# Low parts of a seven-product unit's weight sums in one operation, and three more down units by seven products

## The chip, the cores and the metric

The kernel runs on one core of a Trainium2 chip. The metric is the device time of one execution in microseconds (us). The kernel before took 2016.33 us in the median of 3 runs (2015.55 to 2018.14).

## What is computed

A decoder trunk of two layers on 256 tokens with 2048 channels, in float32. Layer 0 mixes tokens by causal pooling, layer 1 by dilated attention with shared keys and values; each layer ends in a gated feed-forward block (FFN) and a layer norm. The change concerns the FFN, cut here to what matters:

```
def conv_ffn(h, w_up, conv_w, conv_b, w_down):
    S = h.shape[1]
    u = h @ w_up                                   # 2048 -> 2 x 5504
    ...
    gate, val = jnp.split(c, 2, axis=-1)           # c: u after a causal convolution of width 3
    return (jax.nn.silu(gate) * val) @ w_down      # 5504 -> 2048
```

## The kernel before

**Numbers in two parts.** The operands of the large products have the type float32r. Each is held as a high part (the number rounded to that type) and a low part (the rest), and a product of two operands is three matmuls: high by high, high by low, low by high. For a weight tile, ScalarE makes the high part `wh` by a copy and VectorE the low part `wl` by a subtraction. In `do_split` these are lines 99 and 100 of the kernel.

**Units.** All large products are cut into units, one unit for each weight tile of 512 rows by 512 columns (1 MB). A unit's life: SyncE's queue loads the tile into `raw` (3 buffers, line 89); the split makes `wh` and `wl` (4 buffers each); TensorE runs the unit's matmuls; post-processing follows where a sum is complete. `run_units` walks the list of units in order. Before the matmuls of unit i it issues loads up to unit i + 5 and the split of unit i + 3 (`ahead`), then the matmuls, then whatever was put off to this unit (`later`), then the post-processing. Each engine takes its own instructions in exactly this order, so the order of `ahead`, pending work and post-processing is the order of VectorE's and of ScalarE's queue.

**Plain units and seven-product units.** An up unit (lines 180 and 181) is 32 matmuls. A plain down unit (`go_t`, lines 255 to 257) is 24 matmuls of 512 columns: 4 blocks of 128 rows, 2 halves of the tokens, 3 matmuls each. A seven-product unit computes the same by a Strassen-like scheme with 7 block products in place of 8: 7 x 2 x 3 = 42 matmuls of 256 columns (lines 244 to 246). It needs sums of blocks of the weight tile and sums of blocks of the left operand, and it is two entries in the list of units:

- part "a" has the load. `split_sums(i, "a")` makes the high part of three blocks (ScalarE, line 119), the low part (VectorE, line 121), and turns the raw tile in place into the four sums of blocks (VectorE, lines 120, 122 and 124). Its matmuls are three of the seven products.
- part "b" has no load. `split_sums(i, "b")` splits these sums, in two halves of 256 columns, N2 and then N1: the high part by ScalarE (line 113), the low part by VectorE (line 114). N2 is complete after line 122, N1 after line 124. Its matmuls are the other four products, N2's first.

The sums of the left operand are made once for each quarter of the hidden units (512 of the 5504) by `left_sums`; the dictionary `sets` says which memory holds them. Products that leave the scheme go through `early_post` (lines 844 to 857), the rest through `tm_post` (lines 869 to 876), both adding to the tile `ht`.

**Which units use it.** In `ffn`, `sevens` says for each quarter q which of the four column groups of `w_down` go by seven products. Before, these are: in both layers quarters 0 to 6 at all columns and quarter 7 of layer 1 at all columns; quarter 7 of layer 0 at columns 0 and 1; quarter 9 of layer 1 at columns 0 and 2. Eight more units of the shared V projection use it too: 72 in all.

**Where they stand.** In each FFN, quarters 0 to 2 and 3 to 5 are woven into up units (`weave`): up, up, seven, up, seven, up, seven, and so on, so that one round is four plain units and three seven-product units (the woven stretches). Quarters 6 and 7 of each column stand together between groups of up units. Quarters 8 to 10 come last: in layer 0 as plain units in another order of operands, in layer 1 as down units that end the kernel, with the last layer norm behind them.

**Names on the other lines.** Line 607 and 608 collect the up products (`u`), lines 616 to 622 are the convolution, 844 to 876 the down products' additions, 901 to 951 the last norm.

Of the kernel before, what the change touches and what calls it, by code (L numbers as in the profile page):

```python
# [9 lines left out]
F32 = mybir.dt.float32  # L10
# [3 lines left out]
OP = mybir.AluOpType  # L14
# [18 lines left out]
def trunk(ctx: ExitStack, tc: tile.TileContext, x, pool_w_in, pool_w_grp, pool_scale, pool_w_out,  # L33
# [3 lines left out]
    V, A, PE = nc.vector, nc.scalar, nc.tensor  # L37
# [53 lines left out]
    def do_split(i):  # L91
        if len(units[i]) > 3:
            return split_sums(i, units[i][3])
        r = raw.pop(i)
        shape = [P, r.shape[1], r.shape[2]]
        wh[i] = wp.tile(shape, F32R, name=f"wh{i}", tag="wh")
        wl[i] = wp.tile(shape, F32R, name=f"wl{i}", tag="wl")
        for j, s in enumerate(pieces(i, r.shape[1])):
            A.copy(wh[i][:, s], r[:, s])  # L99
            V.tensor_tensor(wl[i][:, s], r[:, s], wh[i][:, s].bitcast(F32), OP.subtract)  # L100
            if i == 0 and j == 0:
                x_quad(0, (1,))


    B1, B2, N1, N2 = slice(0, 4, 2), slice(1, 4, 2), slice(256, 512), slice(0, 256)

    def split_sums(i, kind):
        h = wh[i] = wp.tile([P, 4, 512], F32R, name=f"wh{i}", tag="wh")
        l = wl[i] = wp.tile([P, 4, 512], F32R, name=f"wl{i}", tag="wl")
        if kind == "b":  # L110
            r = raw.pop(i - 1)
            for n in (N2, N1):
                A.copy(h[:, :, n], r[:, :, n])  # L113
                V.tensor_tensor(l[:, :, n], r[:, :, n], h[:, :, n].bitcast(F32), OP.subtract)  # L114
            return
        r = raw[i]
        r11, r12, r22 = r[:, B1, N1], r[:, B1, N2], r[:, B2, N2]
        hs, ls, rs = (t.rearrange("p (k b) n -> p k (b n)", b=2)[:, :, 256:] for t in (h, l, r))
        A.copy(hs, rs)  # L119
        V.tensor_tensor(r12, r12, r11, OP.subtract)  # L120
        V.tensor_tensor(ls, rs, hs.bitcast(F32), OP.subtract)  # L121
        V.tensor_tensor(r22, r22, r12, OP.subtract)  # L122
        both = r[:, :, N1].rearrange("p (k b) n -> p k b n", b=2)
        V.tensor_tensor(both, both, r22.unsqueeze(2).to_broadcast([P, 2, 2, 256]), OP.subtract)  # L124
# [455 lines left out]
    def ffn(lay):  # L580
# [5 lines left out]
        sevens = {q: every for q in range(8)}  # L586
        sets = {0: "C", 1: "A", 2: "B", 3: "C", 4: "A", 5: "B", 6: "A", 7: "CB"[lay], 9: "A"}
        if lay == 1:
            sevens[9] = (0, 2)
        else:  # L590
            sevens[7] = (0, 1)
        free, done = {}, {}

        def pads():
# [265 lines left out]
    def tm_post(lay, n, c):  # L860
# [92 lines left out]
        return post  # L953

    ffn(0)
    marks.append(len(units))

# [174 lines left out]
    add_last(attn_w_o[0], rows4, [lambda j=j: oq[j] for j in range(4)], True, 1, 0, after=to_tokens)  # L1132
    marks.append(len(units))
    ffn(1)
    marks.append(len(units))

# [34 lines left out]
    with tc.tile_pool(name="pool", bufs=1) as pp:  # L1171
# [5 lines left out]
        for l in range(2):  # L1177
            n = 80 if l == 0 else 64
            r = pp.tile([80, P], F32, name=f"vrow{l}")
# [94 lines left out]
```

## Time and profile before

| | |
|---|---|
| profiled execution, span | 2014.9 us |
| median of 3 runs | 2016.33 us |
| TensorE matmul busy | 2005.8 us, 12760 instructions |
| VectorE busy | 1734.9 us, 1831 instructions |
| ScalarE busy | 1269.7 us, 1551 instructions |
| DMA moved | 407.77 MB, mean 202 GB/s |

How to read it: the profile is one execution on the chip, and its span runs from the first to the last instruction. PE is TensorE's matmul, PEld its weight load, DVE VectorE, ACT ScalarE, POOL GpSimd, SP SyncE, which issues the loads. A matmul's row lasts longer than its share of the time, since matmuls overlap; what counts is the distance from one start to the next. "Idle before" is idle time of the engine ahead of an instruction, and the arrow names what ended it. A row of a timeline gives the start, the length, the engine, the line, the operation and the tiles (written from read).

### The profile page before, as it was taken

The numbers are of one execution on the slowest core, as the hardware profiler recorded it, in microseconds if no ns is written. First come the engines' busy times: TensorE is split into PE (matmuls) and PEld (weight loads), VectorE is DVE, ScalarE is ACT, GpSimd is POOL, SyncE is SP. The second block draws the span as 40 slices with busy tenths as digits, with TensorE's granted clock in tenths as the row PEclk, the third lists the DMA queues.
The fourth block names the chain that finished last, engine by engine and source line by source line (L and its number), as shares of the span: only waits on it lengthen the run. The fifth ranks groups of instructions, "written<-read, shape, count | busy, mean of one in ns | idle before, by whom it ended". The sixth has DMA issues, their size and how long they took to land.

```text
span 2014.9 us, 31474 instructions
## 1 busy us (share of the span) xinstructions
PE 2005.8 (100%) x12760; PEld 1810.2 (90%) x12760; DVE 1734.9 (86%) x1831; ACT 1269.7 (63%) x1551; POOL 93.0 (5%) x153
## 2 busy tenths in 40 slices
PE   9999999999999999999999999999999999999999
PEld 8898988999899988889888988998899989989987
DVE  6868887999899899879896878787899899989899
ACT  6454686767766676657554445487766677667673
POOL 2000000000000000000001021000000000000000
PEclk9999999999999999999999999999999999999999
DMA  8565466666666757885465656557666756666765
GB/s 260 204 208 186 163 212 192 181 221 223 198 198 200 239 179 229 232 230 186 155 220 172 210 172 202 187 188 211 166 224 200 224 186 222 209 211 186 213 208 185
DMA packets 271297, 407.77 MB, mean 202 GB/s; under 512 B 74430, under 2 KB 85588, under 8 KB 270896
## 3 DMA queue, kind: packets, MB, share of 16 engines
q1 hardware_dynamic: 259488, 388.93, 58.8%
q0 software_dynamic: 11232, 16.18, 5.4%
q8 instruction: 100, 1.64, 0.3%
q10 hardware_dynamic: 432, 0.66, 0.1%
q14 instruction: 45, 0.37, 0.1%
HBM read 380.01 MB, written 2.10 MB: 190 GB/s over the span
## 4 chain that ended last, share of the span: by engine, by line
PE 88%; DVE 7%; ACT 2%; DMA 2%; issue 1%; SPq 0%; DVEq 0%; ACTq 0%
PE acc L180 41%; PE acc L181 21%; PE s L244 3%; PE s L246 3%; PE s L245 3%; PE acc L184 2%; PE acc L185 2%; PE acc L183 2%; PE t L246 2%; PE t L244 2%; PE t L245 2%; DVE wl L100 2%; ACT wh L99 1%; DVE wl L114 1%; DVE wl L121 1%
## 5 line engine op out<-in xcount | busy, mean ns | idle before, releaser
L180 PE MATMUL acc<-xc,wh 128*128 128x512 f32 x3264 | 1151.6, 396 | 0.0
L181 PE MATMUL acc<-xc,wl 128*128 128x256 f32 x3264 | 916.2, 281 | 0.8 <-DVE wl L100 0.8
L100 DVE TENSOR_TENSOR wl<-raw,wh 128x2048 fp32r<-128x2048 f32 (+2 forms) x304 | 654.8, 2162 | 171.0 <-ACT wh L99 163.3
L180 PEld LDWEIGHTS acc<-xc,wh 128*128 128x128 f32 x3264 | 616.1, 189 | 142.8 <-issue 0.4
L99 ACT CAST wh<-raw 128x2048 fp32r<-128x2048 f32 (+2 forms) x304 | 546.6, 1805 | 170.8 <-PE acc L180 65.7
L181 PEld LDWEIGHTS acc<-xc,wl 128*128 128x128 f32 x3264 | 615.2, 188 | 1.3 <-DVE wl L100 1.2
L113 ACT CAST wh<-raw 128x1024 fp32r<-128x1024 f32 x144 | 150.7, 1052 | 202.8 <-DVE raw L122 175.5
L114 DVE TENSOR_TENSOR wl<-raw,wh 128x1024 fp32r<-128x1024 f32 x144 | 171.8, 1221 | 11.2 <-ACT wh L113 11.2
L121 DVE TENSOR_TENSOR wl<-raw,wh 128x1536 fp32r<-128x1536 f32 x72 | 126.2, 1753 | 6.3 <-ACT wh L119 5.3
L119 ACT CAST wh<-raw 128x1536 fp32r<-128x1536 f32 x72 | 106.4, 1477 | 36.6 <-PE acc L180 26.5
L287 POOL DMA_DIRECT2D ht<-w x48 | 41.3, 1015 | 1446.4 <-DVE ht L873 720.9
L244 PE MATMUL t<-wh,g 128*128 128x256 f32 x376 | 105.8, 281 | 0.0
L246 PE MATMUL t<-wh,g 128*128 128x256 f32 x376 | 105.7, 281 | 0.0
L245 PE MATMUL t<-wl,g 128*128 128x256 f32 x376 | 105.5, 281 | 0.0
L616 ACT ACTIVATE c<-u,cv 128x256 f32<-128x256 f32 x172 | 89.5, 593 | 23.2 <-DVE f L678 16.5
L246 PE MATMUL s<-wh,xs 128*128 128x256 f32 x344 | 96.1, 279 | 0.0
L244 PE MATMUL s<-wh,xs 128*128 128x256 f32 x344 | 95.9, 279 | 0.0
L245 PE MATMUL s<-wl,xs 128*128 128x256 f32 x344 | 95.9, 279 | 0.0
L124 DVE TENSOR_TENSOR raw<-raw 128x1024 f32<-128x1024 f32 x72 | 88.2, 1225 | 2.4
L621 ACT ACTIVATE a<-u,cv 128x256 f32<-128x256 f32 x172 | 73.5, 500 | 11.9 <-DVE g L688 11.9
L607 ACT COPY u<-acc 128x512 f32<-128x512 f32 x84 | 46.8, 572 | 46.1 <-PE acc L181 45.9
L621 ACT ACTIVATE u<-u,cv 128x256 f32<-128x256 f32 x172 | 73.4, 500 | 0.0
(338 smaller groups left out, 3443.1 us busy)
## 6 DMA issues: line engine op xcount, KB each, us to landing
raw<-in_ffn_w_up_dram SPq DMA_DIRECT2D x160, 1024.0 KB, 5.2
raw<-in_ffn_w_down_dram SPq DMA_DIRECT2D x80, 1024.0 KB, 5.1
raw<-in_pool_w_out_dram SPq DMA_DIRECT2D x16, 1024.0 KB, 5.0
raw<-in_shared_w_k_dram SPq DMA_DIRECT2D x16, 1024.0 KB, 5.2
raw<-in_attn_w_q_dram SPq DMA_DIRECT2D x16, 1024.0 KB, 5.3
raw<-in_shared_w_v_dram SPq DMA_DIRECT2D x16, 1024.0 KB, 5.4
raw<-in_attn_w_o_dram SPq DMA_DIRECT2D x16, 1024.0 KB, 5.2
ht<-w POOLq DMA_DIRECT2D x50, 256.0 KB, 4.8
```

The costliest lines, as they stand in the source:

```text
L99: A.copy(wh[i][:, s], r[:, s])
L100: V.tensor_tensor(wl[i][:, s], r[:, s], wh[i][:, s].bitcast(F32), OP.subtract)
L113: A.copy(h[:, :, n], r[:, :, n])
L114: V.tensor_tensor(l[:, :, n], r[:, :, n], h[:, :, n].bitcast(F32), OP.subtract)
L119: A.copy(hs, rs)
L121: V.tensor_tensor(ls, rs, hs.bitcast(F32), OP.subtract)
L180: PE.matmul(ps[m].ap, h[:, k, c], q[:, k, :, :T], start=st, stop=False)
L181: PE.matmul(ps[m][:, :T], l[:, k, c], q[:, k, 0, :T], start=False, stop=sp)
L244: PE.matmul(to, xh, h[:, k, n], start=opens and kk == 0, stop=False)
L245: PE.matmul(to, xh, l[:, k, n], start=False, stop=False)
L246: PE.matmul(to, xl, h[:, k, n], start=False, stop=ends and kk == 1)
L621: A.activation(to[:, m, :], u[:, m, i:i + T], AF.Copy, scale=cv[:, i, j:j + 1])
```

## The change

The split of part "b" is done in one operation on each engine instead of two halves, and three more down units go by seven products: quarter 7 of layer 0 at columns 2 and 3, quarter 9 of layer 1 at column 1. With all four columns of quarter 7 of layer 0 so computed, `left_sums` puts the fourth sum of that quarter into the part of the quarter's own tile that is not read any more, as for the other quarters.

```
         if kind == "b":
             r = raw.pop(i - 1)
-            for n in (N2, N1):
-                A.copy(h[:, :, n], r[:, :, n])
-                V.tensor_tensor(l[:, :, n], r[:, :, n], h[:, :, n].bitcast(F32), OP.subtract)
+            A.copy(h, r)
+            V.tensor_tensor(l, r, h.bitcast(F32), OP.subtract)
             return
...
         if lay == 1:
-            sevens[9] = (0, 2)
-        else:
-            sevens[7] = (0, 1)
+            sevens[9] = (0, 1, 2)
```

## The prediction

> **What bounds the kernel now.** I read the page first, then busy time by stretches, then groups of instructions by shape, then the timelines of VectorE, ScalarE and TensorE side by side.
>
> ```profile
> span 2014.9 us, 31474 instructions
> PE 2005.8 (100%) x12760; PEld 1810.2 (90%) x12760; DVE 1734.9 (86%) x1831; ACT 1269.7 (63%) x1551; POOL 93.0 (5%) x153
> ...
> PE 88%; DVE 7%; ACT 2%; DMA 2%; issue 1%; SPq 0%; DVEq 0%; ACTq 0%
> ...
> L181 PE MATMUL acc<-xc,wl 128*128 128x256 f32 x3264 | 916.2, 281 | 0.8 <-DVE wl L100 0.8
> ```
>
> TensorE has hardly a gap (the largest behind the start is the 0.8 us of the last row, where it waited for VectorE's L100), and the chain of waits runs through it for 88% of the span. So time is gained only by less TensorE work, and lost wherever another engine delivers late. VectorE's 86% hides how close it is; the stretches show that (columns: length, then busy time and count of PE, PEld, DVE, ACT, POOL, clock, DMA share, GB/s).
>
> ```profile
> 625.27:662.56 37.29, 37.29 (x256) 34.43 (x256) 35.67 (x33) 24.30 (x28) 1.72 (x2) 1.00 0.66 209
> 805.88:811.46 5.58, 5.58 (x27) 4.52 (x26) 3.32 (x5) 3.94 (x6) 0.00 (x0) 1.00 0.56 125
> 811.46:816.41 4.95, 4.95 (x44) 4.95 (x43) 3.11 (x3) 4.71 (x7) 0.00 (x0) 1.00 1.00 259
> ```
>
> The first row is one round of a woven stretch, three seven-product units and four plain ones: VectorE works 35.67 of 37.29 us. The other two are TensorE's time for one plain down unit (5.58) and one seven-product unit (4.95). The second engine has 1.6 us of slack a round.
>
> **The change, part by part.** First the prices, by shape (busy, mean ns, idle before).
>
> ```profile
> L100 DVE TENSOR_TENSOR wl<-raw,wh 128x2048 fp32r<-128x2048 f32 x264 | 602.9, 2289 | 155.8 <-ACT wh L99 151.7 <-ACT wgb L474 1.7 <-PE acc L181 0.6
> L99 ACT CAST wh<-raw 128x2048 fp32r<-128x2048 f32 x264 | 502.3, 1906 | 158.2 <-PE acc L180 62.0 <-issue 23.7 <-DMA raw<-in_ffn_w_down_dram 17.1
> L114 DVE TENSOR_TENSOR wl<-raw,wh 128x1024 fp32r<-128x1024 f32 x144 | 171.8, 1221 | 11.2 <-ACT wh L113 11.2
> L113 ACT CAST wh<-raw 128x1024 fp32r<-128x1024 f32 x144 | 150.7, 1052 | 202.8 <-DVE raw L122 175.5 <-PE t L257 12.3 <-PE acc L180 4.2
> L121 DVE TENSOR_TENSOR wl<-raw,wh 128x1536 fp32r<-128x1536 f32 x72 | 126.2, 1753 | 6.3 <-ACT wh L119 5.3
> L124 DVE TENSOR_TENSOR raw<-raw 128x1024 f32<-128x1024 f32 x72 | 88.2, 1225 | 2.4
> L122 DVE TENSOR_TENSOR raw<-raw 128x512 f32<-128x512 f32 x72 | 49.8, 692 | 2.5
> L120 DVE TENSOR_TENSOR raw<-raw 128x512 f32<-128x512 f32 x72 | 49.2, 683 | 0.0
> ```
>
> *Three units more.* TensorE saves 5.58 - 4.95 = 0.63 us each, 1.9 in all. VectorE adds, back to back, some 0.6 + 1.7 + 0.7 + 1.2 = 4.2 us each (L120 to L124; the last subtraction costs what L100 did). No load is added. In FFN 0 the fourth sum's tile moves into the g tile, by operations of the same shapes, and the last addition of two columns gets half as wide: nothing to 0.3 us each, taken as nothing.
>
> *One operation for two.* The new copy and subtraction have the shape of L99 and L100: 1.91 us for 2 x 1.05, and 2.29 for 2 x 1.22 (back to back about 2.20 for 2.33). So each of the 72 units saves VectorE 0.1 to 0.15 us. But L114 almost never waits today (11.2 us in 144), and ScalarE's L113 does, for L122: the half copy of columns N2 runs while VectorE is still in L124. The whole copy must wait for L124, and the subtraction for the whole copy.
>
> ```profile
> 639.96 1.23 DVE L124 TENSOR_TENSOR raw<-raw 128x1024 f32<-128x1024 f32 x1
> 641.10 2.43 DVE L114 TENSOR_TENSOR wl<-raw,wh 128x1024 fp32r<-128x1024 f32 x2
> 644.11 2.29 DVE L100 TENSOR_TENSOR wl<-raw,wh 128x2048 fp32r<-128x2048 f32 x1 [0.58 <-ACT wh L99]
> ```
>
> ```profile
> 641.22 1.06 ACT L113 CAST wh<-raw 128x1024 fp32r<-128x1024 f32 x1 [0.15 <-DVE raw L124]
> ```
>
> L124 ends at 641.19 and ScalarE's second half starts 0.03 later; a whole copy would run from about 641.24 to 643.15, and the subtraction start at 643.19 instead of 641.10. VectorE takes its queue in order, so it stands still for 2.05 us, with the splits of the next units and the post-processing (L608, L622, the additions to ht) queued behind; TensorE waits for these, and SyncE's queue of loads waits for the raw tile. The subtraction ends 1.9 late. Behind it the 0.58 before L100 goes, since ScalarE's next copy runs under the whole subtraction. Net lateness of VectorE: about 1.3 us.
>
> How often? Where post-processing lies between L124 and L114, it fills the hole:
>
> ```profile
> 431.05 1.23 DVE L124 TENSOR_TENSOR raw<-raw 128x1024 f32<-128x1024 f32 x1
> 432.19 1.22 DVE L622 TENSOR_TENSOR c<-c,a 128x1024 f32<-128x1024 f32 x1
> ...
> 435.76 2.35 DVE L114 TENSOR_TENSOR wl<-raw,wh 128x1024 fp32r<-128x1024 f32 x2
> ```
>
> Going through all 72 pairs on VectorE's timeline, 39 have nothing between (the one at 639.96 among them), 28 of these in the four woven stretches; 16 are filled as here; 17 have some 1.2 us between, which leaves 0.85 to 0.95.
>
> **What of it reaches TensorE.** The lead of a unit is the start of the first matmul that reads wl, less the end of the operation that wrote it. Pairs of rows, VectorE's and TensorE's, where it is short or decides:
>
> ```profile
> 440.43 2.29 DVE L100 TENSOR_TENSOR wl<-raw,wh 128x2048 fp32r<-128x2048 f32 x1
> 492.43 2.41 DVE L114 TENSOR_TENSOR wl<-raw,wh 128x1024 fp32r<-128x1024 f32 x2
> 780.83 2.29 DVE L100 TENSOR_TENSOR wl<-raw,wh 128x2048 fp32r<-128x2048 f32 x1 [1.42 <-ACT wh L99]
> 832.26 2.32 DVE L114 TENSOR_TENSOR wl<-raw,wh 128x1024 fp32r<-128x1024 f32 x2
> 1035.85 2.40 DVE L114 TENSOR_TENSOR wl<-raw,wh 128x1024 fp32r<-128x1024 f32 x2
> 1865.33 2.29 DVE L100 TENSOR_TENSOR wl<-raw,wh 128x2048 fp32r<-128x2048 f32 x1 [1.95 <-ACT wh L99]
> 1921.86 2.35 DVE L114 TENSOR_TENSOR wl<-raw,wh 128x1024 fp32r<-128x1024 f32 x2
> ```
>
> ```profile
> 443.90 0.28 PE L181 MATMUL acc<-xc,wl 128*128 128x256 f32 x1
> 499.42 0.28 PE L245 MATMUL s<-wl,xs 128*128 128x256 f32 x1
> 783.62 0.28 PE L181 MATMUL acc<-xc,wl 128*128 128x256 f32 x1
> 841.09 0.28 PE L245 MATMUL s<-wl,xs 128*128 128x256 f32 x1
> 1036.94 0.28 PE L244 MATMUL s<-wh,vs 128*128 128x256 f32 x1
> 1925.13 0.28 PE L245 MATMUL s<-wl,xs 128*128 128x256 f32 x1
> ```
>
> Leads: 1.2 us (443.90), 4.6 (499.42), 0.5 (783.62), 6.5 (841.09), 0.9 (1925.13); at 1036.94 there is none, the first half of wl being ready at 1037.07, just as it is wanted. (At 1865.33 stands a wait that is used below.)
>
> *Four woven stretches* (351 to 500, 546 to 690, 1436 to 1580, 1631 to 1775). A stretch has four rounds with 1, 2, 2, 2 unfilled pairs. Lateness: 1.3, 3.8, 6.4, 9.0 us, and 9.6 at the last subtraction itself. At 443.90 it is 3.75 against 1.2, so TensorE is 2.6 late; at 499.42 it is 9.6 against 4.6: 5.0. In the plain stretches between, VectorE catches up: after the first there is this.
>
> ```profile
> 509.35 0.42 DVE L845 TENSOR_TENSOR w<-w,s 128x256 f32<-128x256 f32 x1 [2.46 <-ACT w L844]
> ```
>
> So each stretch starts anew: 4 x 5.0 = 20 us.
>
> *FFN 0, quarters 7 and 6* (730 to 860). Fills of 0.85, 0.95, none and 0.95 make VectorE 4.7 late at 783.62, against 0.5: 4.2. The two new units there bring 4.2 + 2.05 each, their waits unfilled, and quarter 6 two times 0.9; idle time takes back some 3:
>
> ```profile
> 813.21 1.76 DVE L100 TENSOR_TENSOR wl<-raw,wh 128x1536 fp32r<-128x1536 f32 x1 [3.38 <-DMA h<-hb]
> ```
>
> 4.7 + 12.5 + 1.8 - 3 = 16 late at 841.09, against 6.5: 9.5, say 9. TensorE's saving lies ahead of this point and is swallowed.
>
> *Shared V, 1020 to 1040.* Two unfilled pairs follow each other with no plain unit between: VectorE is 3.9 late where there is no lead, and the whole wl lands at 1038.25 + 3.9 = 1042.2, wanted at 1037.1: 5, of which TensorE loses 0.8 already: 4.
>
> *FFN 1 from 1818 to the end.* Three unfilled pairs and five with 0.9 give 10.4, of which I let idle pieces like the 1.95 at 1865.33 take back 3: 7.5 late at 1925.13, against 0.9: 6.5. From there VectorE hardly rests:
>
> ```profile
> 1962.34 0.41 DVE L845 TENSOR_TENSOR w<-w,s 128x256 f32<-128x256 f32 x1
> ...
> 1964.44 0.69 DVE L857 TENSOR_TENSOR ht<-ht,s 128x512 f32<-128x512 f32 x1
> ...
> 2004.72 0.41 DVE L876 TENSOR_TENSOR ht<-ht,th 128x256 f32<-128x256 f32 x1
> ```
>
> The unit of quarter 9 at column 1 brings 4.2 us and, being the first seven unit of its column, the early additions too (the rows from L845 to L857: 2.7). The rest is one wait more, of quarter 9 at column 0, less about 1 us of gaps. Column 2's is covered by the additions. 7.5 + 4.2 + 2.7 + 1 = 15 on VectorE, nearly one for one at the end, because it sets the end from 1984 on: 14. TensorE's saving there is worth nothing.
>
> Sum: 20 + 9 + 4 + 14 = 47, so 2014.9 + 47 = 2062 on the span; the median of the runs, 2016.33, stands 1.4 above it: **2063 us**. Bounds: nothing lost if leads swallow every wait; 39 x 2.05 + 17 x 0.9 = 95, and some 15 for the new units, if none does. I stand near the middle because it is worked out from the leads.
>
> **The rivals.** *Leads hold (not slower):* if the copy overlapped L124, or the work between were everywhere as at 431.05, VectorE would only gain, 75 x 0.1 = 7.5 us against 3 x 4.2 added, and TensorE's 1.9 remains: 2014.4. It decides as long as no lead is overdrawn. For it: a fifth of the pairs are filled. Against: the 1.2 and 0.5 us. The Trainium skill, Perfetto Trace Analysis, Optimizing Scalar/DVE Operations, says that grouping into larger operations can help a saturated engine, at some 60 ns per operation for DVE on SBUF, and also that breaking instructions up may let work be completed sooner where they cause bubbles elsewhere. By the first, 75 x 0.06 = 4.5 us would leave VectorE and the kernel end at this rival's time; the rows agree on the saving (0.1), and the second is my forecast.
>
> *Half of it is swallowed:* VectorE's idle pieces (0.58, 1.42 and the like) may give back more than I counted, some 1 us per round: 47 less 16 in the weaves and 8 elsewhere leaves 23: 2039.
>
> *More is late:* the raw tile is held 2 us longer, so loads start later; half a microsecond a round is 6 us in the weaves, and the same in the other stretches and gaps that I counted as caught up, 15 more: 2084. Longer TensorE waits might also slow its clock. With gaps of 0.8 us the clock stays at 1.00 here, so no run shows that. The Trainium skill, TensorE: Matmul & The Clock Gate, warns of gaps over about 3 us.
>
> **How the numbers follow.** Forecast (2040 to 2084) 0.83, half swallowed (2022 to 2040) 0.07, more late 0.05, leads hold 0.05. Range: from 2034, inside the second case, to 2084. What a measurement can tell is about 0.2%, 4 us. Slower by more: 0.95; the last case is no change (0.04), with a little left for faster (0.01).
>
> **What would show it.** In the new profile the subtraction at the place of L114 should wait for ScalarE some 100 us in all, about 2 us at a time; TensorE should show gaps before L181, L245 and in the last stretch; each woven stretch 5 us longer, the last 190 us 14 longer. Wrong it is if VectorE's wait stays under 30 us, or if TensorE stays without gaps though VectorE waits.

## The result, and the profile after

The changed kernel takes **2097.15 us** in the median of 4 runs (2096.24 to 2097.87); the kernel before, on the same chip, 2016.34 us (2015.55 to 2018.14). The ratio is 1.040, with a 95% interval of 1.0386 to 1.0414. The profiled execution has a span of 2095.1 us, 80.2 more than before. The forecast was 2063 us, at most 2084: the direction was right, and the loss nearly twice as large.

From the changed kernel's page: the busy times, the chain of waits, and four of the costliest groups. The lines behind the edit have moved up: L112 and L113 are the one copy and the one subtraction, L123 is the old L124, L244 the old L245.

```profile
span 2095.1 us, 31465 instructions
...
PE 2035.5 (97%) x12814; PEld 1825.3 (87%) x12814; DVE 1742.6 (83%) x1776; ACT 1259.8 (60%) x1483; POOL 93.1 (4%) x153
...
PE 42%; DVE 34%; ACT 10%; issue 8%; DMA 6%; SPq 0%; ACTq 0%; DVEq 0%
...
L180 PE MATMUL acc<-xc,wl 128*128 128x256 f32 x3264 | 918.4, 281 | 9.7 <-DVE wl L100 9.3
L112 ACT CAST wh<-raw 128x2048 fp32r<-128x2048 f32 x75 | 143.1, 1909 | 310.0 <-DVE raw L123 281.4
L113 DVE TENSOR_TENSOR wl<-raw,wh 128x2048 fp32r<-128x2048 f32 x75 | 171.8, 2290 | 106.6 <-ACT wh L112 106.6
L244 PE MATMUL s<-wl,xs 128*128 128x256 f32 x362 | 107.9, 298 | 27.3 <-DVE wl L113 27.3
```

The wait that was foretold is there: VectorE stands still 106.6 us before the subtraction, in place of 11.2, because ScalarE's whole copy has to wait for the last sum. The chain of waits has left TensorE: 42% in place of 88%, VectorE 34% in place of 7%. VectorE's busy share has fallen from 86 to 83%; it got slower by standing still.

Where the time went is read from the start of the same unit's first matmul in both traces. From TensorE's timeline of the kernel before, in order: the first plain unit behind the first woven stretch (L180), then for the second, the third and the fourth stretch its first seven-product unit (L244) and the first plain unit behind it (L180).

```profile
502.10 0.39 PE L180 MATMUL acc<-xc,wh 128*128 128x512 f32 x1
558.32 0.28 PE L244 MATMUL s<-wh,g 128*128 128x256 f32 x1
696.31 0.39 PE L180 MATMUL acc<-xc,wh 128*128 128x512 f32 x1
1449.33 0.28 PE L244 MATMUL s<-wh,g 128*128 128x256 f32 x1
1587.34 0.39 PE L180 MATMUL acc<-xc,wh 128*128 128x512 f32 x1
1643.52 0.28 PE L244 MATMUL s<-wh,g 128*128 128x256 f32 x1
1781.53 0.39 PE L180 MATMUL acc<-xc,wh 128*128 128x512 f32 x1
```

The same units in the changed kernel:

```profile
507.95 0.50 PE L179 MATMUL acc<-xc,wh 128*128 128x512 f32 x1
564.80 0.28 PE L243 MATMUL s<-wh,g 128*128 128x256 f32 x1
711.98 0.50 PE L179 MATMUL acc<-xc,wh 128*128 128x512 f32 x1
1488.02 0.28 PE L243 MATMUL s<-wh,g 128*128 128x256 f32 x1
1635.77 0.49 PE L179 MATMUL acc<-xc,wh 128*128 128x512 f32 x1
1694.00 0.28 PE L243 MATMUL s<-wh,g 128*128 128x256 f32 x1
1842.97 0.49 PE L179 MATMUL acc<-xc,wh 128*128 128x512 f32 x1
```

The differences row by row are 5.85, 6.48, 15.67, 38.69, 48.43, 50.48 and 61.44 us: how late TensorE is at that unit (0.1 at the start of the first stretch). Read off in the same way at the other borders, the loss falls on the prediction's terms like this:

| part (times of before) | forecast | measured |
|---|---|---|
| the four woven stretches | 4 x 5 = 20 | 5.9 + 9.2 + 9.7 + 11.0 = 35.7 |
| plain units between these parts | 0 | 5.2 |
| layer 0, quarters 7 and 6, and what follows to 861 | 9 | 14.2 |
| shared V | 4 | 7.0 |
| layer 1 from 1826 to the end | 14 | 18.0 |
| sum | 47 | 80.2 |

### The profile page after: what moved, and what is told of

It reads as the page before. It is cut to its first block, busy times and chain, and to the rows that moved or that the text cites. A ratio compares the mean times of both kernels' runs of the same rounds, so it can differ in the third digit from the quotient of the medians.

```text
span 2095.1 us, 31465 instructions
## 1 busy us (share of the span) xinstructions
PE 2035.5 (97%) x12814; PEld 1825.3 (87%) x12814; DVE 1742.6 (83%) x1776; ACT 1259.8 (60%) x1483; POOL 93.1 (4%) x153
## 4 chain that ended last, share of the span: by engine, by line
PE 42%; DVE 34%; ACT 10%; issue 8%; DMA 6%; SPq 0%; ACTq 0%; DVEq 0%
PE acc L179 20%; PE acc L180 10%; DVE wl L100 8%; DVE wl L120 5%; ACT wh L112 4%; DMA raw<-in_ffn_w_down_dram 4%; DVE wl L113 4%; DVE raw L123 3%; DVE c L619 3%; PE acc L184 2%; PE acc L183 2%; PE acc L182 2%; ACT wh L99 2%; DVE raw L121 2%; DMA raw<-in_ffn_w_up_dram 2%
## 5 line engine op out<-in xcount | busy, mean ns | idle before, releaser
L180 PE MATMUL acc<-xc,wl 128*128 128x256 f32 x3264 | 918.4, 281 | 9.7 <-DVE wl L100 9.3
L100 DVE TENSOR_TENSOR wl<-raw,wh 128x2048 fp32r<-128x2048 f32 (+2 forms) x301 | 647.9, 2159 | 144.5 <-ACT wh L99 143.1
L99 ACT CAST wh<-raw 128x2048 fp32r<-128x2048 f32 (+2 forms) x301 | 540.7, 1804 | 181.5 <-PE acc L179 71.6
L180 PEld LDWEIGHTS acc<-xc,wl 128*128 128x128 f32 x3264 | 615.6, 189 | 16.6 <-DVE wl L100 16.5
L112 ACT CAST wh<-raw 128x2048 fp32r<-128x2048 f32 x75 | 143.1, 1909 | 310.0 <-DVE raw L123 281.4
L113 DVE TENSOR_TENSOR wl<-raw,wh 128x2048 fp32r<-128x2048 f32 x75 | 171.8, 2290 | 106.6 <-ACT wh L112 106.6
L244 PE MATMUL s<-wl,xs 128*128 128x256 f32 x362 | 107.9, 298 | 27.3 <-DVE wl L113 27.3
L243 PE MATMUL t<-wh,g 128*128 128x256 f32 x396 | 112.8, 285 | 0.0
L245 PE MATMUL t<-wh,g 128*128 128x256 f32 x396 | 112.3, 284 | 0.0
L244 PE MATMUL t<-wl,g 128*128 128x256 f32 x396 | 111.9, 283 | 0.0
L243 PE MATMUL s<-wh,xs 128*128 128x256 f32 x362 | 103.2, 285 | 4.1 <-ACT wh L112 4.1
L245 PE MATMUL s<-wh,xs 128*128 128x256 f32 x362 | 103.2, 285 | 0.0
L244 PEld LDWEIGHTS s<-wl,xs 128*128 128x128 f32 x362 | 70.1, 194 | 35.1 <-DVE wl L113 34.3
L123 DVE TENSOR_TENSOR raw<-raw 128x1024 f32<-128x1024 f32 x75 | 91.9, 1225 | 2.6
L243 PEld LDWEIGHTS t<-wh,g 128*128 128x128 f32 x396 | 75.6, 191 | 0.4
```

Of the source, the lines that this page charges most:

```text
L112: A.copy(h, r)
L113: V.tensor_tensor(l, r, h.bitcast(F32), OP.subtract)
L180: PE.matmul(ps[m][:, :T], l[:, k, c], q[:, k, 0, :T], start=False, stop=sp)
L243: PE.matmul(to, xh, h[:, k, n], start=opens and kk == 0, stop=False)
L244: PE.matmul(to, xh, l[:, k, n], start=False, stop=False)
L245: PE.matmul(to, xl, h[:, k, n], start=False, stop=ends and kk == 1)
```

## The experiments

The theories. **W**: the price is the hole behind the last sum, in which VectorE waits for ScalarE. **U**: it is the three more units. **G**, called O in the second group: it is the coarser grain of one whole operation, wherever it stands. For the sizes, **S** is the prediction's own step, that each woven stretch starts anew, and **C** its rival, that lateness is carried from one stretch into the next. Times are medians; ratios are to the kernel before, run beside them (2016.46 to 2016.77 us).

**The two halves of the change, each alone.** First the one operation, with the units as before:

```
-            for n in (N2, N1):
-                A.copy(h[:, :, n], r[:, :, n])
-                V.tensor_tensor(l[:, :, n], r[:, :, n], h[:, :, n].bitcast(F32), OP.subtract)
+            A.copy(h, r)
+            V.tensor_tensor(l, r, h.bitcast(F32), OP.subtract)
```

> The one-operation split alone, without the three more seven-product units. Theory W (VectorE stands still for about 2.05 us behind its last weight sum, until ScalarE has copied the whole tile, in the 39 pairs with nothing between, and what it loses is hardly given back): 62 of the 81 us, so about 2078 us (2068 to 2090), with some 95 to 105 us of waits before the subtraction. Rival U (the three more units overload VectorE and do most of it): under 2040 us. Rival G (TensorE loses because the low part arrives as one whole and not by halves): 2078 us too, this run does not tell it from W.

2082.72 us, 1.0324 (1.0309 to 1.0339). Then the three units, with halves:

```
-            sevens[9] = (0, 2)
-        else:
-            sevens[7] = (0, 1)
+            sevens[9] = (0, 1, 2)
```

> The three more seven-product units alone, split by halves as before. Theory W: no standing still; in FFN 0 leads of 6 us and idle time cover the two units and TensorE gains 1.3 us there; in the last stretch VectorE gets 4.2 + 2.7 us more with no slack, so 3 to 7 us lost there: 2020 us (2014 to 2026). Rival U: over 2060 us. Rival G: 2020 us, as W.

2026.77 us, 1.0050 (1.0035 to 1.0065). U falls: the one operation costs 66 us by itself, the units 10 (somewhat over the range of W). Both together cost 80.8, some 4 more than the 76 of the two halves. From the groups by shape of the first kernel:

```profile
L100 DVE TENSOR_TENSOR wl<-raw,wh 128x2048 fp32r<-128x2048 f32 x264 | 603.0, 2288 | 140.3 <-ACT wh L99 137.5 <-DMA h<-hb 1.5 <-PE cT L1203 0.3
L113 DVE TENSOR_TENSOR wl<-raw,wh 128x2048 fp32r<-128x2048 f32 x72 | 165.0, 2291 | 104.4 <-ACT wh L112 104.4
```

Against the rows of before, VectorE waits 93.2 us more ahead of the subtraction, 15.5 less ahead of L100, and works 6.8 less: 70.9 net. The kernel lost 66. VectorE's span is always its working time plus its idle time, so the two figures had to be near each other unless its other waits changed; they say that these other waits gave back only some 5 to 7 us (7 by the profiled spans). Nearly nothing is swallowed.

**Less of the hole, the same grain.** ScalarE copies by halves, VectorE subtracts once:

```
             for n in (N2, N1):
                 A.copy(h[:, :, n], r[:, :, n])
-                V.tensor_tensor(l[:, :, n], r[:, :, n], h[:, :, n].bitcast(F32), OP.subtract)
+            V.tensor_tensor(l, r, h.bitcast(F32), OP.subtract)
```

> Units as before; ScalarE copies by halves as before (N2 ahead of the last weight sum's end), VectorE subtracts in one operation. Theory W: VectorE waits only for the second half copy, about 1.1 us instead of 2.05, and the 0.58 us that it waited before the next plain unit's subtraction goes, so the net loss in an unfilled pair is about 0.4 us instead of 1.3; 7 such in a woven stretch are 3 us, near the leads: 2024 us (2016 to 2038). Rival G: the low part comes as one whole here as well, so the loss is that of the one operation on both engines: about 2078 us.

2038.37 us, 1.0107 (1.0090 to 1.0123); two runs took some 2035 us and two 2041, and the last section has their clocks.

**The hole, with the fine grain.** Halves as before, but N1, which is complete last, goes first:

```
-            for n in (N2, N1):
+            for n in (N1, N2):
```

> Units as before, both engines by halves as before, but the half that needs the last weight sum (N1) goes first. Theory W: ScalarE can start only behind the last weight sum; VectorE waits 1.1 us for the first half copy and 0.7 us before the next plain unit's subtraction, net about 1.25 us in an unfilled pair, nearly the 1.3 of the one operation, although the operations are halves: 2072 us (2050 to 2090). Rival G: halves arrive as halves; only their order is the wrong one for the first product, at most 1.2 us a pair where the lead is under 1.2 us: under 2035 us.

2057.62 us, 1.0203 (1.0186 to 1.0220). Two operations in place of one, and still a loss of 41 us: G falls in both. The first came out just over W's range, the second well inside it. (N1 first also delays the half that the first product needs; G allowed for that, and put it under 2035 us.) The rows, of the half copies and then of N1 first:

```profile
L100 DVE TENSOR_TENSOR wl<-raw,wh 128x2048 fp32r<-128x2048 f32 x264 | 602.9, 2288 | 137.4 <-ACT wh L99 134.7 <-ACT wgb L474 1.7
L114 DVE TENSOR_TENSOR wl<-raw,wh 128x2048 fp32r<-128x2048 f32 x72 | 164.9, 2290 | 59.8 <-ACT wh L113 58.7 <-PE acc L180 1.1
```

```profile
L100 DVE TENSOR_TENSOR wl<-raw,wh 128x2048 fp32r<-128x2048 f32 x264 | 603.1, 2289 | 151.9 <-ACT wh L99 150.9
L114 DVE TENSOR_TENSOR wl<-raw,wh 128x1024 fp32r<-128x1024 f32 x144 | 169.9, 1222 | 56.5 <-ACT wh L113 56.4
```

Nearly the same new wait, twice the loss. The other two terms say why: with half copies VectorE gets 18.4 us back at L100 and 6.9 of its own work, net 48.6 - 25.3 = 23.3, measured 22; with N1 first it gets 3.9 and 1.9 back, net 45.3 - 5.8 = 39.5, measured 41.

**Carried, or anew?** One operation in the first woven stretch alone:

```
-            for n in (N2, N1):
+            state["b"] = state.get("b", -1) + 1
+            for n in (slice(0, 512),) if state["b"] < 12 else (N2, N1):
```

> The split of part b in one operation only in the twelve pairs of the first woven stretch; everything else as before. Theory C (the lateness of VectorE is carried: the idle pieces of the plain stretch behind the weave are chains between VectorE and ScalarE that go along with TensorE, not slack): TensorE loses 5.7 us in the first stretch, VectorE stays 9.9 us late through the plain stretch and the second weave, and where the leads there were 0.5 to 1.0 us TensorE loses the rest: 9.4 in all, 2026 us (2023 to 2029), TensorE first short of tiles again in the second weave, although its splits are as before. Theory S (each stretch starts anew, as the prediction had it): 5.7, so 2022 us (2020 to 2023), and no gap of TensorE in the second weave.

2026.30 us, 1.0047 (1.0034 to 1.0059): 9.6 us lost, as C has it; S falls. In the trace the first stretch makes TensorE 5.7 us later, the plain units behind it 0.9 more, and the second stretch, whose own splits are as before, 2.4. From TensorE's timeline of this kernel, in the second stretch:

```profile
579.33 0.39 PE L246 MATMUL s<-wl,xs 128*128 128x256 f32 x1 [0.46 <-DVE wl L115]
...
583.94 0.39 PE L182 MATMUL acc<-xc,wl 128*128 128x256 f32 x1 [1.40 <-DVE wl L100]
```

From 591 on nothing more is lost: the lead has been used up once, and then TensorE is late by all but 1 us of what VectorE is (9.0 us of 10.0, counted from the start of the first stretch). The granted clock is 1.00 all through both stretches, so it has no part in this. Why VectorE did not catch up in the plain stretch is on its timeline in the changed kernel, and then on ScalarE's:

```profile
502.79 2.29 DVE L113 TENSOR_TENSOR wl<-raw,wh 128x2048 fp32r<-128x2048 f32 x1 [2.05 <-ACT wh L112]
...
519.28 0.42 DVE L842 TENSOR_TENSOR w<-w,s 128x256 f32<-128x256 f32 x1 [2.46 <-ACT w L841]
...
528.85 2.29 DVE L100 TENSOR_TENSOR wl<-raw,wh 128x2048 fp32r<-128x2048 f32 x1 [0.57 <-ACT wh L99]
```

```profile
516.92 2.08 ACT L613 ACTIVATE c<-u,cv 128x256 f32<-128x256 f32 x4 [4.08 <-DVE f L675]
518.90 0.35 ACT L841 COPY w<-s 128x256 f32<-128x256 f32 x1
```

VectorE is 9.9 us later here than before, and the idle 2.46 us, which the prediction took for a sign of catching up, stand there unchanged. They are not slack: ScalarE itself has waited for VectorE's tile f (L675), then does four operations of the convolution and copies the tile w, and VectorE waits for that copy. A late VectorE makes ScalarE late, and the wait moves along with both.

**One operation where the hole is filled, and where it is not.** The sixteen pairs with other work between, and then the 28 woven pairs with none (the list gives places among the twelve of a stretch):

```
+WHOLE = [w + k for w in (0, 12, 38, 50) for k in (1, 3, 6, 9)]
...
-            for n in (N2, N1):
+            state["b"] = state.get("b", -1) + 1
+            for n in (slice(0, 512),) if state["b"] in WHOLE else (N2, N1):
```

> One operation only in the 16 pairs of the woven stretches where VectorE has other work between the last sum and the subtraction; everything else as before. Theory W (only the hole costs): no hole, no cost: 2016 us (2014 to 2019). Theory O (the whole-tile operation itself costs, by its coarser grain, wherever it stands): 16 of 72 pairs of the 66 us that all 72 cost: 15, so 2031 us (2024 to 2038).

2016.39 us, 0.9997 (0.9988 to 1.0006). The sixteen subtractions don't wait, and nothing is lost:

```profile
L116 DVE TENSOR_TENSOR wl<-raw,wh 128x2048 fp32r<-128x2048 f32 x16 | 36.5, 2283 | 0.0
```

For the 28 pairs the edit differs in the list alone:

```
+WHOLE = [w + k for w in (0, 12, 38, 50) for k in (2, 4, 5, 7, 8, 10, 11)]
```

> One operation only in the 28 pairs of the woven stretches with nothing between the last sum and the subtraction; everything else as before. Theory W with the lateness carried from the first stretch of each layer into the second: some 19 us in each layer, 2054 us (2046 to 2060). With each stretch starting anew: 4 times 5.7 = 23, 2039 us (2035 to 2044). Theory O, by count: 28 of 72 of 66 us, 26, 2042 us.

2056.48 us, 1.0194 (1.0179 to 1.0210): W, and again the carried size (some 19 us in each layer), not 4 x 5.7. The granted clock is 1.00 here from 30 us on.

**The same 28 pairs, the same operations, another order.** Both operations are put off until the next plain unit has been split:

```
     def do_split(i):
...
+        if state.get("late"):
+            state.pop("late")()
...
+            if state["b"] in WHOLE:
+                def whole():
+                    A.copy(h, r)
+                    V.tensor_tensor(l, r, h.bitcast(F32), OP.subtract)
+                state["late"] = whole
+                return
```

The same edit also moves a load: `ahead(i)` now issues the load of unit i + 5 behind the splits and not ahead of them.

> The same 28 pairs in one operation, but both operations are issued behind the split of the plain unit that follows, so that VectorE has that unit's subtraction (2.3 us) to do while ScalarE copies the whole tile; the loads are issued behind the splits for this. Theory W: the hole is filled, nothing or little is lost: 2018 us (2014 to 2024), the wait of the whole subtraction for the copy near nothing in these 28 pairs. Theory O (coarser grain): as without the change of order, about 2054 us. In between if the tile, which lands 2.3 us later, is itself late for its matmuls.

2020.45 us, 1.0019 (1.0010 to 1.0028); nine of ten runs lie between 2018.09 and 2023.30, and one took 4598.78 us, for which nothing here gives a reason. The whole subtraction's group in the kernel with the 28 pairs, and then in this one, with VectorE's timeline of one pair:

```profile
L116 DVE TENSOR_TENSOR wl<-raw,wh 128x2048 fp32r<-128x2048 f32 x28 | 64.2, 2292 | 57.1 <-ACT wh L115 57.1
```

```profile
L119 DVE TENSOR_TENSOR wl<-raw,wh 128x2048 fp32r<-128x2048 f32 x28 | 63.9, 2284 | 0.0
```

```profile
445.01 1.23 DVE L134 TENSOR_TENSOR raw<-raw 128x1024 f32<-128x1024 f32 x1
446.16 2.28 DVE L101 TENSOR_TENSOR wl<-raw,wh 128x2048 fp32r<-128x2048 f32 x1
448.36 2.28 DVE L119 TENSOR_TENSOR wl<-raw,wh 128x2048 fp32r<-128x2048 f32 x1
```

57.1 us of waiting become none, and 36 of the 40 us lost come back by a change of order alone, with the operations the same: this settles W for these pairs. (The moved load has no run of its own.) Of the 4 us that stay, the trace shows 2 in the second stretch, where TensorE waits for VectorE again; that the tile is ready some 2.2 us later (448.36 in place of 446.16) is the likely reason, without a run of its own. It is no better than the kernel before, since TensorE was its limit.

**The new units, layer by layer**, with halves (first without the last layer's edit, then without the first's):

```
             sevens[9] = (0, 2)
-        else:
-            sevens[7] = (0, 1)
```

> Low parts by halves as before; of the three new units only the two of layer 0 (quarter 7 at columns 2 and 3). Theory A (VectorE's 8.4 us more for them come out at the end of layer 0, where the layer norm's sums and the last splits are on VectorE, as the profile with all three units shows 6.0 us of lateness by there, 1.7 of it from a stretch at half clock): 2022 us (2018 to 2024). Theory B (the leads there hold and TensorE keeps its 1.3 us): 2015 us.

2020.66 us, 1.0018 (1.0008 to 1.0027).

```
-            sevens[9] = (0, 2)
+            sevens[9] = (0, 1, 2)
```

> Low parts by halves as before; of the three new units only the one of layer 1 (quarter 9 at column 1). Theory A (VectorE sets the end from about 1984 on, and gets 4.2 us for the unit and 2.7 for the early additions): 2021 us (2018 to 2024), with a gap of TensorE before the last plain units. Theory B (nothing reaches the end): 2016 us.

2025.32 us, 1.0040 (1.0026 to 1.0054). The last unit alone costs 9 us, somewhat more than A's range; the two of layer 0 cost 4 in place of saving 1.3. From TensorE's timelines, of the first and then of the second:

```profile
890.90 0.55 PE L384 MATMUL shift<-S,ones 128*128 128x256 f32 x1 [2.60 <-DVE S L367]
```

```profile
1991.46 0.80 PE L256 MATMUL t<-wl,g 128*128 128x512 f32 x1 [2.35 <-DVE wl L100]
```

The two units make VectorE late for the sums of the next layer norm (L367 to L384), a place that the prediction had not counted. TensorE gets 4.2 us later there: the 2.60 of this wait, and 5 us at a granted clock of 0.66 behind it (890 to 895), which is 1.7 us of full clock.

**Late down tiles in the third stretch.** There ScalarE waits for loads in the changed kernel and not in the one with the one operation alone. From the instructions on the raw tiles in that stretch, of the one operation alone and then of the changed kernel (us, times; the landing of all raw loads there):

```profile
  DMA raw<-in_ffn_w_down_dram: 0.8, 3
...
DMA to landing us min/median/max: 4.9/5.5/6.7
```

```profile
  DMA raw<-in_ffn_w_down_dram: 8.0, 6
...
DMA to landing us min/median/max: 4.8/6.2/7.3
```

> The changed kernel once more, for a second execution's trace. If the late raw tiles of the third woven stretch (ScalarE waited 8.0 us in six places there for loads that took 6.2 us, against 0.8 us and 5.5 in the kernel with the one operation alone) belong to the kernel, they are there again; if to the execution, ScalarE waits under 2 us there and that stretch grows by about 6 us and not by 9.7. The granted clock falls to a half behind the same waits again (near 768, 871, 1075, 1898 and 1997 us) if the waits bring it on.

A second execution took 2094.43 us. The wait was there again (7.4 us, landing 6.2), and so were the places of half clock, so both belong to the kernel. For the buffers:

```
     def do_split(i):
+        if len(marks) > 1 and i == marks[1]:
+            for k in range(2):
+                for nm in ("wh", "wl"):
+                    wp.tile([P, 4, 512], F32R, name=f"skip{nm}{k}", tag=nm)
```

> The changed kernel with two buffers of wh and of wl skipped between layer 0 and layer 1, so that the buffers fall on the units of layer 1 as they do in the kernel with the one operation alone (two more units of layer 0 have moved them on by two). Theory P (the 7 to 8 us that ScalarE waits for down tiles in the third woven stretch come from which buffer lies beside which): that wait falls under 2 us, the stretch grows by 6 us in place of 9.7, 2092 us. Theory N (not from that): the wait stays at 7 to 8 us and the time at 2097 us.

2097.25 us, 1.0403 (1.0385 to 1.0420), the wait 5.6 us: P is not borne out. Why these loads land later stays open.

## Why the prediction was right in kind and wrong in size

*The wait: right.* About 100 us, 2.05 at a time; it was 106.6. VectorE's lateness at the end of the first stretch was foretold as 9.6 us and came to 10.1, TensorE's as 5.0 and came to 5.9. TensorE's gaps stood before L180 and L244 (the old L181 and L245), as said.

*The failed step: "In the plain stretches between, VectorE catches up ... So each stretch starts anew."* It does not. Only the first of two stretches has a lead to spend. The second one gives nearly the whole of VectorE's 10 us to TensorE: 9.2 in the changed kernel, 9.8 in the kernel with the 28 pairs. The plain units between the parts lose another 5.2 us, where the forecast had nothing. Between the layers the lead does come back: in the kernel with the 28 pairs the third stretch loses 5.7 us again (TensorE is 21.4 us late at its first seven-product unit and 27.1 behind it), as the first one does. The prediction stood "near the middle" between 0 and 110 because it used leads as if they were refilled. A sum without them is nearer: new waits, less what falls away ahead of the next subtraction, less work saved. Read from the traces after the runs it gives 70.9, 38.1 (28 pairs), 23.3, 39.5 and 11.7 (first stretch) where 66, 40, 22, 41 and 9.6 us were lost. As said above, this is an account of VectorE's time and not a test; what it shows is that VectorE's other waits hardly shrank in any of the five.

*FFN 0's quarters 7 and 6, shared V, the end: 27 foretold, 39 measured.* Of the 12 more, up to 10 are TensorE's clock. From the view by stretches of the changed kernel (columns as in the prediction; the granted clock is the third number from the end):

```profile
768.00:772.00 4.00, 4.00 (x21) 4.00 (x22) 2.59 (x2) 4.00 (x6) 0.00 (x0) 0.57 0.72 254
870.00:875.00 5.00, 4.93 (x27) 4.84 (x28) 4.44 (x5) 4.33 (x8) 0.00 (x0) 0.66 0.72 192
1075.00:1080.00 5.00, 5.00 (x29) 4.82 (x28) 3.85 (x2) 1.18 (x2) 0.00 (x0) 0.66 0.88 307
1898.00:1906.00 8.00, 7.12 (x32) 6.84 (x33) 6.53 (x5) 8.00 (x12) 0.00 (x0) 0.57 0.66 225
1997.00:2001.00 4.00, 3.58 (x18) 3.58 (x19) 3.44 (x4) 4.00 (x7) 0.00 (x0) 0.57 0.55 153
```

4 x 0.43 + 5 x 0.34 + 5 x 0.34 + 8 x 0.43 + 4 x 0.43 = 10.3 us of full clock are missing in these five places, all in these three parts. That is an upper bound of their price, since VectorE gains on TensorE meanwhile. The prediction named the possibility under "more is late" and gave it no price.

*"More is late", 2084 at a chance of 0.05,* was the nearest case: late loads (8.0 us of ScalarE's waiting in the third stretch, though they took longer to land, where the case had them start later), other stretches that had been counted as caught up, and the clock all came about, and the price was still too low. (Half a microsecond in each of the sixteen rounds would also have been 8 us, not 6.)

*The three units.* That TensorE's saving "is worth nothing" was right; the two of layer 0 and the last one, each without the merged operation, lose 4 and 9 us.

*"Leads hold" and "half of it is swallowed"* fell: the one operation alone lost 66 us, and VectorE's other waits gave back only some 5 to 7. The Trainium skill's page Perfetto Trace Analysis, Optimizing Scalar/DVE Operations, on which the first drew, says that grouping can help a saturated engine; here it saved VectorE 6.8 us of work and brought it 93.2 us of waiting.

*Left over:* of the 33 us that the forecast lacked, 16 lie in the woven stretches (the carried lateness, the late tiles, and a fresh stretch that costs 5.7 and not 5.0) and 5 between them, up to 10 are the clock; some 2 are not placed.

## What to carry to other kernels

A lead is spent once, not once per stretch: before you let it swallow a wait, show where the late engine really gains on the engine it feeds, and idle time that ends on a third engine is no such place. When the second engine is this close to the first, add up its new waits, what falls away behind them and the work saved, and expect that net at the end unless you can name the wait that will shrink; in these five kernels it came within 5 us. And merging two operations may join two dependencies: the first half was ready early, and with work between producer and consumer the same merged operation cost nothing (16 pairs) or 4 us in place of 40 (28 pairs).

## What the runs showed of the hardware

TensorE's clock can halve behind short waits that lie close together. From TensorE's timeline of the changed kernel:

```profile
867.75 0.39 PE L243 MATMUL s<-wh,xs 128*128 128x256 f32 x1 [1.70 <-ACT wh L112]
870.07 0.38 PE L244 MATMUL s<-wl,xs 128*128 128x256 f32 x1 [1.94 <-DVE wl L113]
...
870.88 0.41 PE L244 MATMUL s<-wl,xs 128*128 128x256 f32 x1
871.09 0.41 PE L245 MATMUL s<-wh,xs 128*128 128x256 f32 x1
```

Two waits of 1.70 and 1.94 us with one matmul between, and 0.8 us later matmuls follow each other every 0.21 us, where 0.12 is usual, for 3.4 us. At 1075 it was 1.72 and 1.94, and at 768, 1898 and 1997 a wait of 0.65, 0.61 or 1.12 and one of 1.94; single waits of 1.70 us (at 802 and 2041) left the clock alone. Single waits of 2.60 and 2.35 us, in the kernels with the two units and with the last one, brought it on; one of 2.34 us with all three units and one of 3.01 us with half copies did not in the profiled executions, so the length of one wait doesn't decide it. Nor does such a pair always: in the kernel with the one operation alone, waits of 0.59 and 1.94 us (1883 to 1886) left the clock at 1.00. What decides it stays open. Of the four runs of the kernel with half copies two had a mean clock of 1.000 and took 2035.06 and 2035.54 us, two had 0.996 and took 2041.19 and 2041.41. The Trainium skill, TensorE: Matmul & The Clock Gate, under "HAM oscillation — how this bites in real kernels", gives as the rule no idle gaps over about 3.4 us; here two waits of 2.5 to 3.7 us together were enough in five places, in two executions of the same kernel, and no gap of it there was over 1.94.
